# Feed-forward weight parts stored with their column blocks interleaved, the interleave changing from unit to unit

## The chip, the core and the metric

One NeuronCore of a Trainium2 chip runs the whole kernel. The metric is device time in microseconds (us) of one execution. The time of the kernel before is 2009.88 us, the median of two runs (2009.18 and 2010.57 us).

## What is computed

A trunk of two layers works on a residual stream of 512 tokens by 1024 channels, all in float32. Cut to what matters:

```python
for layer in range(2):
    h = h + 0.5 * swiglu(rms_norm(h, ffn1_g), ffn1_wg, ffn1_wu, ffn1_wd)    # 1024 -> 2816 -> 1024
    h = h + mixer(rms_norm(h, mix_g))       # layer 0: two kinds of attention; layer 1: gating and convolution
    h = h + 0.5 * swiglu(rms_norm(h, ffn2_g), ffn2_wg, ffn2_wu, ffn2_wd)
    h = h + sigmoid(rms_norm(h, ple_g) @ ple_wgate) * (p[layer] @ ple_wproj)

def swiglu(x, w_gate, w_up, w_down):
    return (silu(x @ w_gate) * (x @ w_up)) @ w_down
```

So there are four feed-forward blocks, with three weight matrices each, and they are most of the work.

## The kernel before, in words

**Three products for one.** The residual stream lies channel by channel in eight tiles `hT[k]` (128 channels by 512 tokens). A float32 product is made of three matmuls in the type float32r: each operand is split into a part that float32r holds (`hi`) and what is left (`lo`), and `mm3` (line 278; the matmuls are lines 281, 282 and 283) adds hi·hi, hi·lo and lo·hi into one bank of PSUM. In the feed-forward blocks the weights are the stationary operand (128 columns, loaded by a LDWEIGHTS in front of each matmul) and the activations are the moving one (512 columns). So `mm3` there loads `whi`, `whi` again, and `wlo`.

**Weights in units.** `wunit` (line 426) makes a `Unit` (line 383): one DMA of 1 MB brings a piece of a weight matrix into a `raw` tile (two buffers). For the gate and up matrices a unit is all 8 blocks of 128 rows by 256 columns; for the down matrix it is 4 blocks of rows by 512 columns (the last one of a group only 2 blocks). Each unit is cut into two parts of 1024 floats a partition, and `split1` (line 399) splits each part: ScalarE casts it to a `whi` tile (`acopy`, whose instruction is line 297), and VectorE subtracts that from the raw part into a `wlo` tile (`tsub`, line 321). There are six buffers of `whi` and six of `wlo`, each of 1024 floats. `pick` (line 405) gives the 128 columns of a part that a matmul takes as its stationary operand; they lie one behind the other in the buffer, at a step of 4 bytes.

**Two ways to cut a unit.** Units with 8 blocks of rows are cut by columns (`by_cols`): part 0 holds the first 128 columns of all 8 blocks, part 1 the other 128. The other units are cut by rows: part 0 holds the first half of the blocks of rows, part 1 the second half.

**Feed-forward loop** (`ffn`, line 587). For each of 11 column groups `j` there are a gate unit and an up unit, and four accumulations (gate 0, gate 1, up 0, up 1), each of 8 `mm3`. `accum` (line 558) runs the first four blocks of rows of each job that it is given, and then the second four; for `j` = 0 it is given all four jobs at once, otherwise one job after the other. Then VectorE and ScalarE multiply, apply silu and split the result into `a` tiles. After 6 and after 11 groups `down` (line 565) multiplies these by the down matrix into two groups of four banks, adds them to `hT`, and the second time feeds the next norm. `down` is also what multiplies by the output matrices of the two mixers. The very first gate and up unit are a `FirstUnit`, which loads and splits them in halves by rows.

**Order.** All instructions are recorded with an engine and an estimated cost. `Plan.order` then sets one order for each engine by a simulation with these costs and with the number of buffers of each kind (`SLOTS`, line 32; limits per stream in `CAPS`, for PSUM six of the eight banks for the main stream). An instruction that takes a new buffer waits for the last reader of the old content. Each engine works its own queue strictly in that order, and waits on semaphores where its data is not there yet.

Of the kernel before, what the change touches and what calls it, by code (L numbers as in the profile page):

```python
# [12 lines left out]
F32 = mybir.dt.float32  # L13
# [7 lines left out]
KD = D // 128  # L21
# [15 lines left out]
class Store:  # L37


    def __init__(self, tag, shape, dt, stream):  # L40
        self.tag, self.shape, self.dt, self.stream = tag, list(shape), dt, stream
        self.writer, self.readers, self.left, self.slot, self.real = None, [], 0, None, None
        self.end = 0.0


class View:
# [14 lines left out]
    def flat(self):  # L61
        p, n = self.arr.shape[0], "abc"[:self.arr.ndim - 1]
        pattern = f"p {' '.join(n)} -> p ({' '.join(n)})"
        return View(self.store, np.broadcast_to(np.False_, (p, self.n)), self.steps + (("rearrange", (pattern,)),))

    def ap(self):
        x = self.store.real
        for name, args in self.steps:
            x = getattr(x, name)(*args)
        return x  # L70

    @property
# [185 lines left out]
def trunk(ctx: ExitStack, tc: tile.TileContext, A: dict, out: bass.AP):  # L258
# [37 lines left out]
    def acopy(o, x):  # L296
        P.op("ACT", 0.83 * o.n + (52.0 if x.psum else 93.0), lambda: nc.scalar.copy(ap(o), ap(x)), w=[o], r=[x])  # L297
# [13 lines left out]
    def dve(o, fn, r, per=1.04, extra=(), fixed=0.0):  # L311
        P.op("DVE", per * o.n + 67.0 + fixed, fn, w=[o] + list(extra), r=r)
# [4 lines left out]
    def tadd(o, a, b):  # L317
        dve(o, lambda: nc.vector.tensor_add(ap(o), ap(a), ap(b)), [a, b])

    def tsub(o, a, b):  # L320
        dve(o, lambda: nc.vector.tensor_sub(ap(o), ap(a), ap(b)), [a, b])  # L321
# [23 lines left out]
    def dma(o, x, kb, after=None):  # L345
        P.op("SP", max(500.0, kb * 2.7), lambda: nc.sync.dma_start(ap(o), ap(x)), w=[o], r=[x, after],
             lat=2000.0 if isinstance(x, View) and isinstance(o, View) else 2000.0)
# [4 lines left out]
    def ps(shape=(128, S)):  # L352
        return P.tile("ps", shape)
# [29 lines left out]
    class Unit:  # L383


        def __init__(self, srcs, k, cols, by_cols):
            raw = P.tile("raw", (128, k, cols))
            for c0, c1, src in srcs:
                dma(raw[:, :, c0:c1], src, 0.5 * k * (c1 - c0))
            self.by_cols, self.half = by_cols, cols // 2 if by_cols else (k + 1) // 2  # L390
            h = self.half
            self.split([raw[:, :, h * i:h * (i + 1)] if by_cols else raw[:, h * i:h * (i + 1), :] for i in range(2)])
# [5 lines left out]

        def split1(self, r):
            hi, lo = P.tile("whi", r.arr.shape, F32R), P.tile("wlo", r.arr.shape, F32R)  # L400
            acopy(hi, r)
            tsub(lo, r, hi.bitcast(F32))
            self.parts.append((hi, lo))

        def pick(self, k, c0, n=128):
            i, r = divmod(c0 if self.by_cols else k, self.half)
            if self.by_cols:
                c0 = r
            else:
                k = r  # L410
            hi, lo = self.parts[i]
            return hi[:, k, c0:c0 + n], lo[:, k, c0:c0 + n]

    class FirstUnit(Unit):


        def __init__(self, w, cols):
            self.w, self.cols, self.by_cols, self.half, self.raw, self.parts = w, cols, False, KD // 2, [], []

        def load(self, tag):  # L420
            r = P.tile(tag, (128, self.half, self.cols))
            k0 = 128 * self.half * len(self.raw)
            dma(r, self.w[k0:k0 + 128 * self.half, 0:self.cols].rearrange("(k p) c -> p k c", p=128), 512)
            self.raw.append(r)

    def wunit(w, k0, k, c0, cols):
        src = w[128 * k0:128 * (k0 + k), c0:c0 + cols].rearrange("(k p) c -> p k c", p=128)
        return Unit([(0, cols, src)], k, cols, k == KD)


    ident = const_tile("ident", [128, 128])
# [22 lines left out]
    for part in (GAINS[:1], GAINS[1:]):  # L454
        rows = 16 * len(part)
        grow = tt(shape=(rows, 128))
        for i, name in enumerate(part):
            src = A[name].rearrange("l (k p) -> (l k) p", p=128)
            P.op("ACT", 60.0, lambda grow=grow, i=i, src=src: nc.scalar.dma_start(ap(grow[16 * i:16 * i + 16, :]), src),
                 w=[grow], lat=(3500.0, 15000.0)[len(gcol)])  # L460
        gcol.append(const_tile(f"gcol{len(gcol)}", [128, rows]))
        with P.on("norm", 60 * (len(gcol) - 1)):
            p = ps()
# [101 lines left out]
    def down(w, cats, k0, scale, norm=None):  # L565
        n = len(cats)
        for mg in range(2):
            accs = [ps() for _ in range(4)]
            for kg in range(0, n, 4):
                kk = min(4, n - kg)  # L570
                u = wunit(w, k0 + kg, kk, 512 * mg, 512)
                for k in range(kk):
                    for m in range(4):
                        mm3(accs[m], u.pick(k, 128 * m), cats[kg + k], kg + k == 0, kg + k == n - 1)
            for m in range(4):
                h = hT[4 * mg + m]
                if scale == 1.0:
                    tadd(h, accs[m], h)
                else:
                    stt(h, accs[m], scale, h, OP.mult, OP.add)  # L580
                if norm is not None:
                    norm.feed(4 * mg + m)
            if norm is not None:
                for m in range(4):
                    norm.stat(4 * mg + m)

    def ffn(pre, layer, norm, nxt, hook=None, first=None):
        xs, rcol, rb = norm.finish()
        wg, wu, wd = A[pre + "_wg"][layer], A[pre + "_wu"][layer], A[pre + "_wd"][layer]
        for j0, j1 in ((0, 6), (6, 11)):  # L590
            cats = []
            for j in range(j0, j1):
                if j == 0 and first is not None:
                    ug, uu = first
                else:
                    ug = wunit(wg, 0, KD, 256 * j, 256)
                    uu = wunit(wu, 0, KD, 256 * j, 256)
                if hook is not None and j == 7:
                    box["gate"] = cats[-1][0]
                    with P.on("hook", HOOK_BIAS):  # L600
                        hook()
                pgs, pus = [ps(), ps()], [ps(), ps()]
                jobs = [(pgs[s], ug, 128 * s) for s in range(2)] + [(pus[s], uu, 128 * s) for s in range(2)]
                if j == 0:
                    accum(xs, jobs)
                else:
                    for job in jobs:
                        accum(xs, [job])
                for pg, pu in zip(pgs, pus):
                    g, a = tt(), tt()  # L610
                    tmul(g, pg, rb)
                    act(g, g, AF.Silu)
                    tmul(a, pu, g)
                    tmul(a, a, rb)
                    cats.append(split(a, at))
            down(wd, cats, 2 * j0, 0.5, nxt if j1 == 11 else None)
# [156 lines left out]
    def even_mixer(norm, nxt, cos, sin):  # L773
        w = A["ev_w_in"][0]
# [59 lines left out]
        wv = w.rearrange("(k p) c -> p k c", p=128)  # L834

        def values(grp):
            accs = [ps() for _ in range(NT)]
            for kg in range(2):
                kw = wv[:, 4 * kg:4 * kg + 4, :]
                if grp == 0:  # L840
                    u = Unit([(0, 4, kw[:, :, 1024:1028]), (4, 258, kw[:, :, 2052:2306])], 4, 258, False)
                else:
                    u = Unit([(0, 258, kw[:, :, 2306:2564])], 4, 258, False)
                for k in range(4):
                    for t in range(NT):
                        mm3(accs[t][:, 0:258], tok(xs[4 * kg + k], t), u.pick(k, 0, 258), kg + k == 0, kg == 1 and k == 3)
            return accs
# [1 line left out]

        P.stream = "mp"  # L850
        u0 = wunit(w, 0, KD, 704, 256)
        u1 = Unit([(0, 64, wv[:, :, 512:576]), (64, 128, wv[:, :, 960:1024]), (128, 256, wv[:, :, 576:704])], KD, 256, True)
        p4 = [ps() for _ in range(4)]
        accum(xs, [(p4[0], u0, 0), (p4[1], u0, 128), (p4[2], u1, 0), (p4[3], u1, 128)])
        with P.on("side", SIDE_BIAS):
# [1 line left out]
        kk = rope(p4[2], 3, krow)  # L857
        iq = [rope(p4[0], None), rope(p4[1], None)]
        with P.on("side", SIDE_BIAS):
# [12 lines left out]
            for t in range(NT):  # L872
                p = ps()
# [11 lines left out]
        with P.on("sc", SC_BIAS):  # L885

            score = [None]
            for t in range(1, NT):
                N = 128 * (t + 1)
                sc = at()  # L890
                for h in range(4):
                    p = ps()
# [30 lines left out]
        for g in range(2):  # L923
            for j in range(2):
                u = wunit(w, 0, KD, 1028 + 512 * g + 256 * j, 256)
                for s in range(2):
                    i = 4 * g + 2 * j + s
                    p = ps()
# [45 lines left out]
        with P.on("aq", AQ_BIAS):  # L974
# [3 lines left out]
            for j in range(2):  # L978
                u = wunit(w, 0, KD, 256 * j, 256)
                for s in range(2):  # L980
                    i = 2 * j + s
                    p = ps()
# [5 lines left out]
        with P.on("pvB"):  # L988
            c = ps((128, NT, 4))
# [24 lines left out]
            v, ok, fo = small(NT, 4), small(NT, 4), small(NT, 4)  # L1014
# [3 lines left out]
            r = rsqrt(v.flat(), NT * 4, 2.0 ** -40)  # L1018
# [171 lines left out]
    n = Norm("ffn1_g", 0)  # L1190
    for k in range(KD):
        with P.on("start"):
            p = ps()
# [20 lines left out]
    n = Norm("ffn2_g", 0)  # L1214
# [3 lines left out]
    n = Norm("ffn1_g", 1)  # L1218
# [3 lines left out]
    n = Norm("ffn2_g", 1)  # L1222
# [4 lines left out]

    const.tile([128, PAD // 4], F32, name="pad")
    order = P.order()
# [7 lines left out]
TOPK_BIAS, AQ_BIAS, CONV_BIAS, CONVP_BIAS, PP_BIAS, DTAIL_BIAS, HOOK_BIAS, PE_TAPS = 2000, 450, 3000, -300, 200, -300, 400, 4  # L1237
PP0_BIAS = 600
PAD = 416
LG_BIAS, LGA_BIAS, PVA_BIAS, SIDE_BIAS, SC_BIAS = -100, -100, -300, 0, -200  # L1240
_INS = ["x", "p", "pos", "ffn1_g", "ffn1_wg", "ffn1_wu", "ffn1_wd", "mix_g", "ffn2_g", "ffn2_wg", "ffn2_wu",
        "ffn2_wd", "ple_g", "ple_wgate", "ple_wproj", "ev_w_in", "ev_w_out", "a_q_g", "a_k_g", "a_w_uv",
# [27 lines left out]
```

## Time and profile before

| what | before |
|---|---|
| median of two runs | 2009.88 us |
| the profiled execution | 2010.54 us |
| its span, first to last instruction | 2008.6 us |
| mean granted TensorE clock, share of full | 0.999 |
| PE (matmuls) busy | 1991.3 us, 99% |
| PEld (weight loads) busy | 1630.2 us, 81% |
| DVE (VectorE) busy | 1080.8 us, 54% |
| ACT (ScalarE) busy | 723.2 us, 36% |
| POOL (GpSimd) busy | 13.8 us, 1% |
| DMA | 202.28 MB, mean 101 GB/s |

The span is what the instructions of the program take; about 2 us of the execution lie around it. Busy times are unions of the recorded instructions. Weight loads have a row of their own (PEld) and run beside the matmuls; the recorded end of a matmul is modelled and overlaps the next one, so the distance between starts says more of its cost than its duration. In the rows, L281 is line 281 of the kernel, a tile's buffer number is left out (`whi` for any of the six), `128*128` is the size of the stationary operand and `128x512` that of the moving one.

### The profile page before, as it was taken

How to read it: one execution, taken by the hardware profiler on the slowest of the kernel's cores; microseconds unless marked ns; L12 is line 12 of the kernel's file. 1: busy time of each engine (PE TensorE's matmuls, PEld its weight loads, DVE VectorE, ACT ScalarE, POOL GpSimd, SP SyncE). 2: the span in 40 equal slices, each digit the busy share in tenths (PEclk: the TensorE clock that was granted, in tenths of full speed). 3: DMA queues.
4: the chain of work that ended last, by engine and by line, in shares of the span. 5: the costliest groups of instructions: out<-in, count | busy, mean ns of one | idle time of the engine just before them, and what ended most of it. 6: DMA issues, size and time to landing. Idle time of an engine off the chain costs nothing.

```text
span 2008.6 us, 22735 instructions
## 1 busy us (share of the span) xinstructions
PE 1991.3 (99%) x9154; PEld 1630.2 (81%) x9154; DVE 1080.8 (54%) x1797; ACT 723.2 (36%) x1057; POOL 13.8 (1%) x35
## 2 busy tenths in 40 slices
PE   8999999999999999999999999999999999999999
PEld 7888888888767888888888888888767888888887
DVE  6442464489986544344466443444699744334443
ACT  6322233344756422132254222223425533213232
POOL 0000000000000000000000000000000000000000
PEclk9999999999999999999999999999999999999999
DMA  5323322354330323332233322323333232323222
GB/s 189 105 97 98 108 85 84 94 160 141 96 110 22 104 86 105 94 95 95 95 121 110 105 98 92 105 75 103 107 105 105 84 97 92 105 85 104 95 104 75
DMA packets 164778, 202.28 MB, mean 101 GB/s; under 512 B 9968, under 2 KB 123072, under 8 KB 164672
## 3 DMA queue, kind: packets, MB, share of 16 engines
q1 hardware_dynamic: 164016, 200.38, 31.3%
q8 instruction: 72, 1.18, 0.2%
q0 software_dynamic: 528, 0.41, 0.2%
q14 instruction: 34, 0.28, 0.0%
q10 hardware_dynamic: 128, 0.03, 0.0%
HBM read 185.33 MB, written 6.29 MB: 95 GB/s over the span
## 4 chain that ended last, share of the span: by engine, by line
PE 97%; DVE 1%; ACT 1%; DMA 1%; issue 0%; SPq 0%; ACTq 0%; DVEq 0%
PE ps L281 30%; PE ps L282 30%; PE ps L283 30%; PE ps L276 6%; PE ps L287 1%; DMA whi<-in_x_dram 0%; ACT t L292 0%; ACT t L297 0%; DVE t L962 0%; DVE t L330 0%; DVE wlo L330 0%; DMA t<-t 0%; DVE t L309 0%; DVE wlo L321 0%; DVE a L913 0%
## 5 line engine op out<-in xcount | busy, mean ns | idle before, releaser
L297 ACT CAST whi<-raw 128x1024 fp32r<-128x1024 f32 (+2 forms) x342 | 348.7, 1022 | 976.3 <-PE ps L282 936.7
L321 DVE TENSOR_TENSOR wlo<-raw,whi 128x1024 fp32r<-128x1024 f32 (+2 forms) x342 | 405.1, 1185 | 496.8 <-ACT whi L297 496.0
L281 PE MATMUL ps<-x,whi 128*128 128x512 f32 x1664 | 655.8, 394 | 0.6 <-ACT x L297 0.6
L282 PE MATMUL ps<-x,whi 128*128 128x512 f32 x1664 | 648.7, 390 | 0.6 <-DVE x L321 0.6
L283 PE MATMUL ps<-x,wlo 128*128 128x512 f32 x1664 | 648.8, 390 | 0.0
L281 PEld LDWEIGHTS ps<-x,whi 128*128 128x128 f32 x1664 | 313.1, 188 | 66.2 <-ACT x L297 1.1
L283 PEld LDWEIGHTS ps<-x,wlo 128*128 128x128 f32 x1664 | 312.9, 188 | 65.6
L282 PEld LDWEIGHTS ps<-x,whi 128*128 128x128 f32 x1664 | 313.2, 188 | 65.1 <-DVE x L321 1.2
L281 PE MATMUL ps<-a,whi 128*128 128x512 f32 x832 | 325.1, 391 | 0.0
L282 PE MATMUL ps<-a,whi 128*128 128x512 f32 x832 | 323.9, 389 | 0.0
L283 PE MATMUL ps<-a,wlo 128*128 128x512 f32 x832 | 323.8, 389 | 0.0
L281 PEld LDWEIGHTS ps<-a,whi 128*128 128x128 f32 x832 | 156.3, 188 | 32.8 <-issue 0.5
L283 PEld LDWEIGHTS ps<-a,wlo 128*128 128x128 f32 x832 | 156.2, 188 | 32.6
L282 PEld LDWEIGHTS ps<-a,whi 128*128 128x128 f32 x832 | 156.2, 188 | 32.3 <-DVE a L321 0.7
L315 DVE TENSOR_TENSOR t<-ps,t 128x512 f32<-128x512 f32 x88 | 60.8, 691 | 209.1 <-PE ps L283 208.3
L315 DVE TENSOR_TENSOR t<-ps,rb 128x512 f32<-128x512 f32 x100 | 68.7, 687 | 112.1 <-PE ps L283 109.9
L330 DVE SCALAR_TENSOR_TENSOR a<-a 128x508 f32<-128x508 f32 (+23 forms) x108 | 72.7, 731 | 5.0 <-ACT a L292 4.6
L292 ACT ACTIVATE t<-t 128x512 f32<-128x512 f32 x100 | 62.9, 629 | 22.9 <-DVE t L315 22.8
L297 ACT CAST a<-t 128x512 fp32r<-128x512 f32 x88 | 54.8, 623 | 36.8 <-DVE t L315 36.8
L315 DVE TENSOR_TENSOR t<-t,rb 128x512 f32<-128x512 f32 x92 | 63.2, 687 | 1.2
L321 DVE TENSOR_TENSOR a<-t,a 128x512 fp32r<-128x512 f32 x88 | 60.4, 686 | 5.2 <-ACT a L297 4.8
L276 PE MATMUL ps<-a 128*128 128x512 f32 (+3 forms) x152 | 58.6, 501 | 1.5 <-ACT t L297 0.5
(167 smaller groups left out, 1358.8 us busy)
## 6 DMA issues: line engine op xcount, KB each, us to landing
raw<-in_ffn_wg_dram SPq DMA_DIRECT2D x43, 1024.0 KB, 5.1
raw<-in_ffn_wu_dram SPq DMA_DIRECT2D x43, 1024.0 KB, 5.1
raw<-in_ffn_wd_dram SPq DMA_DIRECT2D x40, 1024.0 KB, 4.9
raw<-in_ple_wgate_dram SPq DMA_DIRECT2D x8, 1024.0 KB, 5.0
raw<-in_od_w_in_dram SPq DMA_DIRECT2D x8, 1024.0 KB, 5.5
raw<-in_ev_w_in_dram SPq DMA_DIRECT2D x7, 1024.0 KB, 5.8
raw<-in_ffn_wd_dram SPq DMA_DIRECT2D x8, 512.0 KB, 3.7
raw<-in_ev_w_out_dram SPq DMA_DIRECT2D x4, 1024.0 KB, 5.3
```

The lines of the kernel that those rows point to most:

```text
L276: P.op("PE", cost, lambda: nc.tensor.matmul(ap(p), ap(a), ap(b), start=start, stop=stop), w=[p], r=[a, b], lat=160.0)
L281: nc.tensor.matmul(q, x, u, start=first, stop=False)
L282: nc.tensor.matmul(q, x, v, start=False, stop=False)
L283: return nc.tensor.matmul(q, y, u, start=False, stop=last)
L287: P.op("PE", 107.0, lambda: nc.tensor.transpose(ap(p), ap(x), ap(idn)), w=[p], r=[x, idn], lat=160.0)
L292: P.op("ACT", cost, lambda: nc.scalar.activation(ap(o), ap(x), func, scale=ap(scale), bias=ap(bias), **({"accum_out": ap(accum)} if accum ...
L297: P.op("ACT", 0.83 * o.n + (52.0 if x.psum else 93.0), lambda: nc.scalar.copy(ap(o), ap(x)), w=[o], r=[x])
L315: dve(o, lambda: nc.vector.tensor_mul(ap(o), ap(a), ap(b)), [a, b])
L321: dve(o, lambda: nc.vector.tensor_sub(ap(o), ap(a), ap(b)), [a, b])
L330: dve(o, lambda: nc.vector.scalar_tensor_tensor(ap(o), ap(a), ap(s), ap(b), op0=op0, op1=op1, **kw()), [a, s, b], extra=[accum] if accum i ...
```

## The change

A part can now be stored woven: its blocks of 128 columns are taken in groups of `s` (2, 4 or 8), and within a group the columns are interleaved, so that column `c` of block `b` lies at `c * s + b`. The cast and the subtraction write that layout (and the subtraction reads `whi` in it), while `raw` is read as it lies. A matmul's stationary operand is then 128 floats at a step of 8, 16 or 32 bytes. The list `WEAVE` says which way is used: for gate and up by `j % 4` (not woven, 2, 4, 8), for `down` by the number of the unit (2, 4, 8, not woven; units with fewer than 4 blocks of rows are not woven).

The constructor's argument `by_cols` is gone, and every unit is now cut by rows.

```diff
+    def woven(self, s, laid):
+
+        n = self.n // (128 * s)
+        order = "n s c" if laid else "n c s"
+        return View(self.store, np.broadcast_to(np.False_, (self.arr.shape[0], n, s, 128)),
+                    self.steps + (("weave", (f"p ({order}) -> p n s c", n, s)),))
...
-        def __init__(self, srcs, k, cols, by_cols):
+        def __init__(self, srcs, k, cols, weave):
+            self.weave = weave
+            by_cols = False
...
         def split1(self, r):
             hi, lo = P.tile("whi", r.arr.shape, F32R), P.tile("wlo", r.arr.shape, F32R)
-            acopy(hi, r)
-            tsub(lo, r, hi.bitcast(F32))
+            if self.weave is None:
+                acopy(hi, r)
+                tsub(lo, r, hi.bitcast(F32))
+            else:
+                s = self.weave
+                x, h, l = r.flat().woven(s, True), hi.flat().woven(s, False), lo.flat().woven(s, False)
+                acopy(h, x)
+                tsub(l, x, h.bitcast(F32))
             self.parts.append((hi, lo))
...
-            return hi[:, k, c0:c0 + n], lo[:, k, c0:c0 + n]
+            if self.weave is None:
+                return hi[:, k, c0:c0 + n], lo[:, k, c0:c0 + n]
+            i, j = divmod((hi.arr.shape[2] * k + c0) // 128, self.weave)
+            return tuple(v.flat().woven(self.weave, False)[:, i, j, :] for v in (hi, lo))
...
-    def wunit(w, k0, k, c0, cols):
+    def wunit(w, k0, k, c0, cols, weave=None):
         src = w[128 * k0:128 * (k0 + k), c0:c0 + cols].rearrange("(k p) c -> p k c", p=128)
-        return Unit([(0, cols, src)], k, cols, k == KD)
+        return Unit([(0, cols, src)], k, cols, weave)
...
-                u = wunit(w, k0 + kg, kk, 512 * mg, 512)
+                u = wunit(w, k0 + kg, kk, 512 * mg, 512, WEAVE[1][(k0 + kg) // 4 % 4] if kk == 4 else None)
...
-                    ug = wunit(wg, 0, KD, 256 * j, 256)
-                    uu = wunit(wu, 0, KD, 256 * j, 256)
+                    ug = wunit(wg, 0, KD, 256 * j, 256, WEAVE[0][j % 4])
+                    uu = wunit(wu, 0, KD, 256 * j, 256, WEAVE[0][j % 4])
...
+WEAVE = [[None, 2, 4, 8], [2, 4, 8, None]]
```

## Rows read from the trace of the kernel before

**Rows 1.** The page: span, busy times, granted clock by slice, chain that ended last.
```profile
span 2008.6 us, 22735 instructions
PE 1991.3 (99%) x9154; PEld 1630.2 (81%) x9154; DVE 1080.8 (54%) x1797; ACT 723.2 (36%) x1057; POOL 13.8 (1%) x35
...
PEclk9999999999999999999999999999999999999999
...
PE 97%; DVE 1%; ACT 1%; DMA 1%; issue 0%; SPq 0%; ACTq 0%; DVEq 0%
PE ps L281 30%; PE ps L282 30%; PE ps L283 30%; PE ps L276 6%; PE ps L287 1%; DMA whi<-in_x_dram 0%; ACT t L292 0%; ACT t L297 0%; DVE t L962 0%; DVE t L330 0%; DVE wlo L330 0%; DMA t<-t 0%; DVE t L309 0%; DVE wlo L321 0%; DVE a L913 0%
```
**Rows 2.** Windows: length, busy us (instructions) by engine, granted clock, DMA share, GB/s.
```profile
30.00:220.00 190.00, 190.00 (x842) 157.38 (x841) 79.11 (x94) 53.42 (x62) 5.02 (x10) 1.00 0.32 105
380.00:660.00 280.00, 273.77 (x1532) 219.23 (x1531) 228.64 (x653) 153.60 (x332) 4.33 (x8) 1.00 0.36 105
1604.00:1965.00 361.00, 361.00 (x1597) 298.98 (x1597) 156.35 (x192) 108.53 (x132) 0.00 (x0) 1.00 0.31 100
```
**Rows 3.** Timeline, PE, inside a down product: start and length, us.
```profile
200.09 0.39 PE L283 MATMUL ps<-a,wlo 128*128 128x512 f32 x1
...
202.81 0.39 PE L283 MATMUL ps<-a,wlo 128*128 128x512 f32 x1
```
**Rows 4.** Timeline, PEld, the same stretch.
```profile
200.10 0.19 PEld L281 LDWEIGHTS ps<-a,whi 128*128 128x128 f32 x1
200.32 0.19 PEld L282 LDWEIGHTS ps<-a,whi 128*128 128x128 f32 x1
```
**Rows 5.** Instruction groups, PE and PEld: count, busy us, mean ns, idle before.
```profile
L281 PE MATMUL ps<-x,whi 128*128 128x512 f32 x1664 | 655.8, 394 | 0.6 <-ACT x L297 0.6
L281 PE MATMUL ps<-a,whi 128*128 128x512 f32 x832 | 325.1, 391 | 0.0
...
L281 PEld LDWEIGHTS ps<-x,whi 128*128 128x128 f32 x1664 | 313.1, 188 | 66.2 <-ACT x L297 1.1 <-issue 0.7 <-DVE t L325 0.3
...
L287 PEld LDWEIGHTS ps<-ident,t 128*128 128x128 f32 x156 | 18.3, 141 | 7.8 <-issue 2.8 <-ACT t L292 1.4 <-DVE t L330 0.6
...
L276 PEld LDWEIGHTS ps<-t,a 128*64 128x64 f32 x160 | 13.0, 136 | 8.5 <-DVE t L309 3.7 <-ACT t L297 1.8 <-DVE s L962 0.9
...
L276 PEld LDWEIGHTS ps<-t,a 128*128 128x128 f32 x80 | 10.9, 191 | 2.8 <-ACT t L297 1.2 <-issue 0.5
```
**Rows 6.** Timeline, PEld, a run of matmuls with one moving column.
```profile
381.72 0.86 PEld L276 LDWEIGHTS ps<-ones,rb 128*128 128x128 f32 x7
```
**Rows 7.** Instruction groups, ACT and DVE: making the parts, emptying PSUM.
```profile
L321 DVE TENSOR_TENSOR wlo<-raw,whi 128x1024 fp32r<-128x1024 f32 x318 | 388.6, 1223 | 483.6 <-ACT whi L297 482.7
L297 ACT CAST whi<-raw 128x1024 fp32r<-128x1024 f32 x318 | 333.8, 1052 | 935.5 <-PE ps L282 895.8 <-PE ps L283 17.8 <-issue 13.1
...
L315 DVE TENSOR_TENSOR t<-ps,t 128x512 f32<-128x512 f32 x88 | 60.8, 691 | 209.1 <-PE ps L283 208.3 <-ACT t L292 0.7
...
L330 DVE SCALAR_TENSOR_TENSOR h<-ps,h 128x512 f32<-128x512 f32 x64 | 42.6, 689 | 14.1 <-PE ps L283 14.1
```
**Rows 8.** Waits: us in total, times, longest us.
```profile
ACT whi L297 <- PE ps L282: 936.7, 261, 11.4
...
DVE t L315 <- PE ps L283: 318.3, 128, 5.6
```
**Rows 9.** Timeline, DVE, around the step between two halves of a down product.
```profile
173.54 1.22 DVE L321 TENSOR_TENSOR wlo<-raw,whi 128x1024 fp32r<-128x1024 f32 x1 [4.21 <-ACT whi L297]
176.04 2.73 DVE L330 SCALAR_TENSOR_TENSOR h<-ps,h 128x512 f32<-128x512 f32 x4 [1.27 <-PE ps L283]
178.94 1.23 DVE L321 TENSOR_TENSOR wlo<-raw,whi 128x1024 fp32r<-128x1024 f32 x1 [0.17 <-ACT whi L297]
```

More of the change, by code (lines that the diff above doesn't have):

```diff
@@ L68, in ap @@
         for name, args in self.steps:
-            x = getattr(x, name)(*args)
+            if name == "weave":
+                x = x.rearrange(args[0], n=args[1], s=args[2], c=128)
+            else:
+                x = getattr(x, name)(*args)
         return x
@@ L400, in split1 @@
             hi, lo = P.tile("whi", r.arr.shape, F32R), P.tile("wlo", r.arr.shape, F32R)
-            acopy(hi, r)
-            tsub(lo, r, hi.bitcast(F32))
+            if self.weave is None:
+                acopy(hi, r)
+                tsub(lo, r, hi.bitcast(F32))
+            else:
+                s = self.weave
+                x, h, l = r.flat().woven(s, True), hi.flat().woven(s, False), lo.flat().woven(s, False)
+                acopy(h, x)
+                tsub(l, x, h.bitcast(F32))
             self.parts.append((hi, lo))
@@ L418, in __init__ @@
             self.w, self.cols, self.by_cols, self.half, self.raw, self.parts = w, cols, False, KD // 2, [], []
+            self.weave = None
         def load(self, tag):
@@ L840, in values @@
                 if grp == 0:
-                    u = Unit([(0, 4, kw[:, :, 1024:1028]), (4, 258, kw[:, :, 2052:2306])], 4, 258, False)
+                    u = Unit([(0, 4, kw[:, :, 1024:1028]), (4, 258, kw[:, :, 2052:2306])], 4, 258, None)
                 else:
-                    u = Unit([(0, 258, kw[:, :, 2306:2564])], 4, 258, False)
+                    u = Unit([(0, 258, kw[:, :, 2306:2564])], 4, 258, None)
                 for k in range(4):
@@ L851, in even_mixer @@
         u0 = wunit(w, 0, KD, 704, 256)
-        u1 = Unit([(0, 64, wv[:, :, 512:576]), (64, 128, wv[:, :, 960:1024]), (128, 256, wv[:, :, 576:704])], KD, 256, True)
+        u1 = Unit([(0, 64, wv[:, :, 512:576]), (64, 128, wv[:, :, 960:1024]), (128, 256, wv[:, :, 576:704])], KD, 256, None)
         p4 = [ps() for _ in range(4)]
```

## The prediction

> **What bounds the kernel now.** I read the page first: PE is busy 99% of the span, the granted clock is at full speed (2.4 GHz) in every slice, and the chain that ended last is 97% PE, nine tenths of it the three lines of `mm3` [rows 1]. So only what changes the distance between matmuls, or makes PE wait, counts. The windows come second: inside the feed-forward blocks PE has no idle time (190.00 of 190.00 us, 842 matmuls), DVE is busy 42% and ACT 28%; in the even mixer PE idles 6 us of 280 and DVE is busy 82% [rows 2].
>
> The timeline then gives the price of one matmul. Twelve steps lie between the two starts shown, 2.72 us, so one float32r matmul of 512 columns takes 226.7 ns from start to start [rows 3]; 190 us over 842 gives 225.7 with the few short ones in it [rows 2]. 512 columns at 2.4 GHz would be 213.3, so 13.4 ns are on top. A weight load starts about 10 ns after the matmul before its own [rows 3, 4] and is recorded with 188 ns [rows 5]. How much of that occupies the load path? A load of 64 columns is recorded with 136 ns, so a column takes (188 - 136) / 64 = 0.81 ns, 128 columns 104 ns, and some 84 ns are latency [rows 5]. Where the moving operand has one column, seven loads fill 0.86 us, so one follows the other after (0.86 - 0.19) / 6 = 112 ns [rows 6]: that is the least period that a load sets, 104 ns of reading and 8 around it. Today the load needs 112 to 122 ns (with the 10 ns of lag) out of 226.7, and is hidden.
>
> **The change, part by part.**
>
> *Which loads change.* Per feed-forward block, `j` % 4 leaves 3 of 11 column groups as they are, 3 have step 8, 3 step 16 and 2 step 32; a group is two units, 96 matmuls. In `down` a full unit has 48 matmuls, and the numbers of the units give, for both column halves, 4 units of step 8, 2 of step 16 and 2 of step 32 per block. The four `down` calls of the mixers go through the same line: 4 units of step 8 and 4 of step 16 in all. Sum: step 8: 4 x 3 x 96 + 16 x 48 + 4 x 48 = 2112 matmuls; step 16: 1152 + 384 + 192 = 1728; step 32: 768 + 384 = 1152; 4992 of the 7488 in these groups (3 x (1664 + 832)) [rows 5]. No matmul, load or byte of DMA is added.
>
> *A load at a step.* No row shows one, so I bound it. From below it costs nothing; a gain can't exceed the 13.4 ns above the columns [rows 3]. From above, if all words between were read too, step 8 takes 2 x 104 ns, step 16 4 x 104, step 32 8 x 104. The period would be 112 + (k - 1) x 104 ns, plus at most 10 of lag, where k is the factor on the reading. k = 2 gives 216 to 226 ns, just under 226.7: hidden. k = 3 gives 320 to 330, k = 4 424 to 434, k = 8 840 to 850. So the whole question is whether the reading at step 16 and 32 takes more than about 2.05 times as long as now. The nearest row is the load in the transposes (L287): the same 128 columns with 141 ns, 47 less than 188, which leaves 57 ns of reading, 0.45 ns a column [rows 5]. It is another kind of load, but it shows that words can come nearly twice as fast as `whi` asks for them; a path with that reserve can lose half its rate and the load is as now. I take k between 1 and 2 for all three steps, because a halved rate is the mildest penalty and two mild ones in a row would still be hidden: 0 us.
>
> [...]
>
> *Casting and subtracting into the woven layout.* Of the 318 parts of 1024, 88 become step 8, 72 step 16 and 48 step 32 (four or two parts per group or unit as counted above). A cast takes 1052 ns and a subtraction 1223 [rows 7]. No row has an operand at a step; lower bound no change, upper bound three times the part that goes with the columns (the whole above some 200 ns): 2.8 and 3.3 us. I take a doubling of that part for steps 16 and 32 and nothing for step 8: +0.86 and +1.08 us on 120 parts, 103 us of ACT and 130 us of DVE, which lifts them to 41% and 60% of the span [rows 1]. What hides it: ACT waits for PE to give up a buffer before 261 casts, 937 us in all [rows 8], so a part is made as soon as the oldest of six buffers is free. A part feeds 24 matmuls, 5.44 us, so five parts or 27 us lie before its use, against 2.3 us now, 4.2 with my value and 6.1 at the upper bound.
>
> The cost that can show is in the queues: whatever stands behind a longer subtraction on DVE, above all what empties PSUM. In the gate and up loop two of six banks are spare, 10.9 us of cover. Between the halves of a down product it is tighter: the four updates of `hT` run from 176.04 us on, one every 0.69 us, and the subtraction before them began at 173.54 [rows 9]. At the upper bound it would begin 1.7 us later and last 3.3, to 178.6, and the first bank come free at 179.3. The third accumulation of the next half wants it 2.04 + 1.36 us after 176.04, at 179.4: still hidden, with nothing to spare; where the next norm is fed in between (once per block), up to a microsecond may show. In the even mixer, with DVE at 82% [rows 2], four parts of step 16 add 4 x 1.08 = 4.3 us to DVE and may show in full. I take +4 us for all of this, between 0 and 15.
>
> *All units cut by rows.* Gate and up units need both parts within 2.7 us of the first matmul instead of 5.4, and give them up at 8.2 and 10.9 us instead of 5.4 and 10.9. With three units in six buffers the next use is still some 22 us off, so this is hidden by the same cover. The instruction count is the same. But the planner sets all queues anew, also where nothing is woven; where PE waits at all (6 us in the even mixer [rows 2]) this can go either way, -5 to +5 us. I take 0.
>
> **Sum.** 0 + 4 + 0 = +4 us on the profiled execution of 2010.54 us, which is 0.7 us above the median 2009.88; on the median 2014 us.
>
> **Rivals.**
>
> B, *the load becomes the bound.* One column at step 16 or 32 takes three times as long as now. Then 2880 matmuls go from 226.7 to some 325 ns: 2880 x 98 = 282 us, 2292 us. It decides from k = 2.05 on, at 4.7 us for each further 0.016 (1.6 ns a matmul). For it: the margin at k = 2 is no more than 0 to 10 ns. Against: the faster loads of L287. [...]
>
> C, *only a part of B.* Step 32 alone goes to k = 3 (1152 x 98 = 113 us, 2123 us), or a halved rate meets the 213 ns of the moving operand and adds 10 ns on 2880 (29 us, 2039 us). Between 2030 and 2150.
>
> D, *worse.* The words in between are read (k = 4 at step 16: 1728 x 202 = 349 us, k = 8 at step 32: 1152 x 618 = 712 us), or step 8 pays as well: 2450 us and more.
>
> E, *the subtractions come late.* The upper bound on DVE and ACT, with a stall of a few us at each of the some 20 joints between products: 2050 us.
>
> F, *faster.* Some of the 13.4 ns comes from reading weights and activations at the same time, and the other addresses avoid it: at most 4992 x 13.4 = 67 us, 1943 us. Nothing in the rows speaks for it: the 13.4 ns are the same in both kinds of product.
>
> **How the numbers follow.** The forecast (all loads hidden, 2000 to 2030 us) gets 0.62, B 0.17, C 0.11, D 0.04, E 0.02, F 0.04. About 2% (40 us) is what a measurement of this kernel tells from no change: faster 0.04; within it the 0.62 and the low end of C, 0.64; slower 0.32. The range has to take in B, because forecast, C and E alone leave a quarter out: from 1998 (forecast with a lucky order) to 2310 (B with its lag). The forecast's own range is 2000 to 2030.
>
> **What would show it.** Right: weight loads of `whi` and `wlo` with groups of 188 ns beside longer ones, none over about 300 (84 + 2 x 104), matmul starts still 226.7 ns apart at every step, PE idle below 20 us, casts and subtractions of two or three lengths up to 1.9 and 2.3 us, and ACT's wait for PE shorter by what the casts grew. B: starts some 325 ns apart and loads near 400 ns in the units of step 16 and 32 and unchanged ones in the rest. E: PE idle before L281 ended by `wlo` or by a bank. The forecast is wrong if starts are over 231 ns apart in any woven unit, or if PE's waits grow by more than 20 us.

## The result, and the profile after

The changed kernel takes 2075.1 us (median of two runs, 2075.02 to 2075.18) against 2009.88: the ratio is 1.032, with a 95% interval of 1.030 to 1.034. It is slower by 65 us. That lies inside the range, but only because the range had been drawn out to take in rivals C and B (up to 2310 us); it is outside the forecast's own 2000 to 2030, and the +4 us of the sum were 65.

The page of the kernel after; its lines stand ten higher from `mm3` on (L281 to L283 are now L291 to L293, L297 is L307, L321 is L331):

```profile
span 2073.2 us, 22760 instructions
PE 2047.8 (99%) x9154; PEld 1793.3 (87%) x9154; DVE 1196.1 (58%) x1802; ACT 860.8 (42%) x1053; POOL 13.8 (1%) x35
...
PEclk9999999999999999999999999999999999999999
...
PE 93%; DVE 4%; DMA 1%; ACT 1%; issue 1%; SPq 0%; DVEq 0%; ACTq 0%
```

Beside [rows 1]: as many matmuls, the same clock (0.998 of full on the mean, 0.999 before), PE busy 99% as before, and 65 us more. The matmuls themselves follow each other more slowly (233 to 244 ns in woven units, against 226.7). The chain has 4% of DVE in it where there was 1%: something waits for VectorE now. Windows split the two. First the even mixer, then a whole feed-forward block (the second of four), then the odd mixer; columns as in [rows 2]. Before the change:

```profile
373.50:651.00 277.50, 271.27 (x1517) 216.80 (x1516) 227.88 (x653) 153.51 (x333) 4.33 (x8) 1.00 0.36 106
651.00:1011.30 360.30, 360.30 (x1597) 298.43 (x1596) 155.29 (x191) 108.30 (x133) 0.00 (x0) 1.00 0.29 95
...
1416.70:1595.50 178.80, 177.83 (x764) 134.67 (x763) 151.91 (x241) 80.31 (x119) 0.40 (x4) 0.99 0.31 104
```

And after it:

```profile
385.00:675.00 290.00, 278.22 (x1518) 225.61 (x1517) 234.28 (x658) 156.19 (x329) 4.33 (x8) 0.99 0.35 101
675.00:1047.00 372.00, 372.00 (x1597) 335.62 (x1596) 181.38 (x192) 140.76 (x133) 0.00 (x0) 1.00 0.29 92
...
1464.00:1648.40 184.40, 180.75 (x762) 140.92 (x762) 155.63 (x241) 84.48 (x119) 0.41 (x4) 0.98 0.30 100
```

The first and the last weight matmul of a block in the timeline give the limits. A block went from 360.2 to 371.9 us with the same 1597 matmuls and no idle PE (the first, with its start-up, from 363.5 to 375.1); the even mixer from 277.5 to 290.0, the odd from 178.8 to 184.6, both with more PE idle. So 46.5 us come from the four blocks and 18.3 from the two mixers: 64.8, and the spans differ by 64.6.

Inside a block the units can be told apart. Windows of 21 us in column groups 1 to 4 of the first block: step 8, 16, 32 bytes, not woven.

```profile
37.00:58.00 21.00, 21.00 (x92) 17.37 (x91) 12.93 (x14) 10.91 (x10) 0.00 (x0) 1.00 0.33 101
59.50:80.50 21.00, 21.00 (x91) 21.00 (x90) 13.83 (x13) 9.61 (x8) 0.00 (x0) 1.00 0.31 101
82.00:103.00 21.00, 21.00 (x87) 21.00 (x87) 8.34 (x12) 6.04 (x8) 0.00 (x0) 1.00 0.30 100
105.00:126.00 21.00, 21.00 (x94) 17.41 (x93) 9.82 (x12) 6.64 (x8) 1.96 (x4) 1.00 0.31 101
```

In the second and third PEld has no gap left (21.00 of 21.00 us), so the load may be the bound there; the sweep below tests it. In the first it has gaps, as in the fourth (17.37 and 17.41 us busy), and yet fewer matmuls fit (92 against 94). The weight loads of these windows, in the same order (mean ns after the bar):

```profile
L292 PEld LDWEIGHTS ps<-x,whi 128*128 128x128 f32 x31 | 6.0, 193 | 1.2
...
L292 PEld LDWEIGHTS ps<-x,whi 128*128 128x128 f32 x30 | 9.3, 310 | 0.0
...
L292 PEld LDWEIGHTS ps<-x,whi 128*128 128x128 f32 x29 | 9.6, 329 | 0.0
...
L292 PEld LDWEIGHTS ps<-x,whi 128*128 128x128 f32 x31 | 5.8, 188 | 1.2
```

188 ns is the value of [rows 5]. Taken from start to start over all units, a matmul takes 226.7 ns where the load has no step, 233.3 at 8 bytes, 235.0 at 16 and 244.4 at 32. With the counts of the prediction (without the mixers' matrices): 1920 x 6.6 + 1536 x 8.3 + 1152 x 17.7 ns = 12.7 + 12.7 + 20.4 = 45.8 us. That is nearly all of the blocks' 46.5.

### The profile page after: what moved, and what is told of

Same layout as the page of the kernel before. It is cut to its first block, busy times and chain, and to the rows that moved or that the text cites. A ratio compares the mean times of both kernels' runs of the same rounds, so it can differ in the third digit from the quotient of the medians.

```text
span 2073.2 us, 22760 instructions
## 1 busy us (share of the span) xinstructions
PE 2047.8 (99%) x9154; PEld 1793.3 (87%) x9154; DVE 1196.1 (58%) x1802; ACT 860.8 (42%) x1053; POOL 13.8 (1%) x35
## 4 chain that ended last, share of the span: by engine, by line
PE 93%; DVE 4%; DMA 1%; ACT 1%; issue 1%; SPq 0%; DVEq 0%; ACTq 0%
PE ps L291 29%; PE ps L292 29%; PE ps L293 29%; PE ps L286 5%; PE ps L297 1%; DVE wlo L331 1%; ACT t L302 0%; DVE a L935 0%; DVE t L984 0%; DVE m L934 0%; SPq L356 0%; DMA whi<-in_x_dram 0%; DMA t<-in_a_w_uv_dram 0%; DVE t L340 0%; DMA t<-t 0%
## 5 line engine op out<-in xcount | busy, mean ns | idle before, releaser
L331 DVE TENSOR_TENSOR wlo<-raw,whi 128x1024 fp32r<-128x1024 f32 (+2 forms) x342 | 513.8, 1503 | 544.5 <-ACT whi L307 544.0
L307 ACT CAST whi<-raw 128x1024 fp32r<-128x1024 f32 (+2 forms) x342 | 484.1, 1419 | 549.2 <-PE ps L292 522.3
L291 PE MATMUL ps<-x,whi 128*128 128x512 f32 x1664 | 667.7, 401 | 1.9 <-ACT x L307 1.9
L292 PE MATMUL ps<-x,whi 128*128 128x512 f32 x1664 | 659.7, 396 | 0.2 <-DVE x L331 0.2
L293 PE MATMUL ps<-x,wlo 128*128 128x512 f32 x1664 | 659.2, 396 | 0.0
L291 PEld LDWEIGHTS ps<-x,whi 128*128 128x128 f32 x1664 | 398.7, 240 | 43.9 <-ACT x L307 2.4
L292 PEld LDWEIGHTS ps<-x,whi 128*128 128x128 f32 x1664 | 398.9, 240 | 41.3 <-issue 1.7
L293 PEld LDWEIGHTS ps<-x,wlo 128*128 128x128 f32 x1664 | 398.7, 240 | 41.3
L291 PE MATMUL ps<-a,whi 128*128 128x512 f32 x832 | 331.6, 399 | 0.0
L292 PE MATMUL ps<-a,whi 128*128 128x512 f32 x832 | 329.1, 396 | 0.0
L293 PE MATMUL ps<-a,wlo 128*128 128x512 f32 x832 | 329.0, 395 | 0.0
L291 PEld LDWEIGHTS ps<-a,whi 128*128 128x128 f32 x832 | 199.0, 239 | 21.4 <-issue 0.9
L292 PEld LDWEIGHTS ps<-a,whi 128*128 128x128 f32 x832 | 199.4, 240 | 20.3
L293 PEld LDWEIGHTS ps<-a,wlo 128*128 128x128 f32 x832 | 199.2, 239 | 20.4
L331 DVE TENSOR_TENSOR a<-t,a 128x512 fp32r<-128x512 f32 x88 | 60.6, 689 | 35.7 <-ACT a L307 35.7
L340 DVE SCALAR_TENSOR_TENSOR a<-a 128x506 f32<-128x506 f32 (+22 forms) x108 | 73.0, 726 | 5.2 <-ACT a L302 4.8
L307 ACT CAST a<-t 128x512 fp32r<-128x512 f32 x88 | 54.7, 622 | 39.5 <-DVE t L325 39.5
```

The lines of the kernel that those rows point to most:

```text
L291: nc.tensor.matmul(q, x, u, start=first, stop=False)
L292: nc.tensor.matmul(q, x, v, start=False, stop=False)
L293: return nc.tensor.matmul(q, y, u, start=False, stop=last)
L340: dve(o, lambda: nc.vector.scalar_tensor_tensor(ap(o), ap(a), ap(s), ap(b), op0=op0, op1=op1, **kw()), [a, s, b], extra=[accum] if accum i ...
```

## The experiments

Two theories on the step: L, the load alone takes longer and becomes the bound; S, the load and the moving operand are read at the same time and delay each other. And on the mixers: the new order of the queues (theory A of the first run), or parts that are made too late (theory B). The changed kernel and the runs without a step, with storing alone, with reading alone and with step 8 bytes everywhere put the instructions of PE, VectorE and ScalarE in the same order, so between these five only the layouts differ.

**Cut by rows, nothing woven.**

```diff
-WEAVE = [[None, 2, 4, 8], [2, 4, 8, None]]
+WEAVE = [[None] * 4, [None] * 4]
```

> Every unit is cut by rows as in the changed kernel, but none is woven. Theory A (the step of the weight loads costs the time in the feed-forward blocks, +11.7 us each, and the new order of the queues the rest): the four blocks fall back to 360.2 us each, matmul starts 226.7 ns apart everywhere, and the mixers keep what they lost, so 2010 + 15 = 2025 us. Theory B (the mixers lose because casts and subtractions at a step are late there): all of it goes, 2007 to 2014 us.

2018.26 us against 2011.01 of the kernel before on the same chip, ratio 1.004 (1.003 to 1.005): +7 us, between the two numbers. Windows of the second block and the even mixer:

```profile
373.30:655.00 281.70, 274.02 (x1517) 217.92 (x1517) 230.90 (x658) 151.94 (x328) 4.34 (x8) 1.00 0.36 104
655.00:1015.30 360.30, 360.30 (x1597) 298.43 (x1596) 157.04 (x191) 109.25 (x133) 0.00 (x0) 1.00 0.30 95
```

The blocks are back at 360.2 us; the even mixer keeps 4.2 us of its 12.5, the odd one 1.2 of 5.8. So the row cut with its new order costs some 5 to 7 us, nearly all of it outside the blocks (the first one takes 0.7 us more), and what the mixers lose beyond that needs the steps.

**Woven in the feed-forward blocks alone**, other units of 8 blocks cut by columns again.

```diff
-            by_cols = False
+            by_cols = k == KD and weave is None
...
-..., WEAVE[1][(k0 + kg) // 4 % 4] if kk == 4 else None)
+..., WEAVE[1][(k0 + kg) // 4 % 4] if kk == 4 and ff else None)
```

> Woven as in the changed kernel in the feed-forward blocks alone; the output matrices of the mixers are not woven, and units of 8 blocks that are not woven are cut by columns as before. Theory A: feed-forward blocks at 371.9 us each as in the changed kernel, mixers close to the kernel before (277.5 and 178.8 us), 2010 + 47 = 2057 us. Theory B: the same time, because no part at a step is made in the mixers; the two are told apart by the other run. A third, that the loss in the mixers follows from any new order by chance: mixers off by some 10 us either way, 2045 to 2070 us.

2057.63 us, ratio 1.023 (1.022 to 1.025), the time that both theories gave. Blocks at 371.9 us, mixers at 278.3 and 180.4. The blocks' loss does not depend on what else was changed.

**Stored woven, read as it lies.**

```diff
         def pick(self, k, c0, n=128):
...
-            if self.weave is None:
-                return hi[:, k, c0:c0 + n], lo[:, k, c0:c0 + n]
-            i, j = divmod((hi.arr.shape[2] * k + c0) // 128, self.weave)
-            return tuple(v.flat().woven(self.weave, False)[:, i, j, :] for v in (hi, lo))
+            return hi[:, k, c0:c0 + n], lo[:, k, c0:c0 + n]
```

> Parts are stored woven as in the changed kernel, but every matmul reads 128 words in a row, so the products of woven units are taken with the wrong weights; instructions and waits are those of the changed kernel. If reading at a step is the cost: weight loads all 188 ns, starts 226.7 ns apart, blocks at 360.2 us, casts still 1.13, 2.06 and 2.23 us, and only the mixers' share remains: 2022 to 2027 us. If storing at a step is (ScalarE's and VectorE's accesses slowing TensorE's reads, or late parts): the blocks stay at 366 us or more, over 2045 us.

2025.92 us, +15, ratio 1.007 (1.005 to 1.010). A window of the second block and its loads:

```profile
659.80:1020.00 360.20, 360.20 (x1596) 298.38 (x1595) 179.88 (x191) 139.15 (x133) 0.00 (x0) 1.00 0.30 95
...
L292 PEld LDWEIGHTS ps<-x,whi 128*128 128x128 f32 x352 | 66.1, 188 | 13.6
```

DVE is as busy as in the changed kernel (180 us of 360) and PE as fast as before the change: storing at a step, and the longer casts and subtractions, cost nothing in the blocks (one of four has a stall of 1.6 us). In the mixers the run takes 286.3 and 183.8 us, 4.6 and 3.8 more than with nothing woven.

**Stored as it lies, read at a step.**

```diff
-            if self.weave is None:
+            if True:
                 acopy(hi, r)
                 tsub(lo, r, hi.bitcast(F32))
```

> Parts are stored as they lie, by casts and subtractions of the old length, and the matmuls of the units that the changed kernel weaves read at the same steps as there, so they multiply the wrong words. Theory (reading at a step costs the time in the blocks; the late casts cost some 8 us in the mixers; the new order some 7): blocks at 371.9 us each, mixers between those of the run with nothing woven and those of the changed kernel, 2010 + 47 + 3 + 7 = 2067 us. If storing at a step had a share in the blocks: below 2055 us.

2068.4 us, ratio 1.028 (1.026 to 1.030). Blocks at 371.9 us (375.8 the first), mixers at 285.2 and 181.0, which is 3.5 and 1.0 above nothing woven. In the mixers the order then costs 4.2 + 1.2, reading 3.5 + 1.0, storing 4.6 + 3.8, in all 18.3 us, and the changed kernel lost 18.3 there.

That close a sum is in part luck, and the split of the mixers is not shown. Each figure comes from one execution, while the ten times of the run with nothing woven lie between 2016 and 2026 us. And the clock differs: the write-only run has a granted clock of 0.50 for 6.8 us of the even mixer and 10.2 of the odd, the changed kernel for 3.4 and 6.8, the read-only run for 3.4 and 3.4, the kernel before and the run with nothing woven for 0 and 3.4. The first such stretch of the changed kernel came right after one in which PE worked only 1.39 of 3.40 us:

```profile
615.70:619.10 3.40, 1.39 (x7) 0.83 (x8) 2.78 (x16) 3.20 (x11) 0.00 (x0) 1.00 0.73 222
619.10:622.50 3.40, 3.40 (x16) 2.68 (x16) 1.94 (x9) 1.66 (x6) 0.00 (x0) 0.50 0.25 89
```

An estimate from the 0.50: where PE sets the pace, half of such a stretch is lost, so up to 6.8 of the 8.4 us put to storing can be the clock, and up to 1.7 of the 4.5 put to reading. The blocks are free of this: the granted clock is 1.00 in every window of a feed-forward block read here.

**A sweep of the load's step, with four kinds of moving operand.**

```diff
+    def swept(f, v, p, u, xs):
+        st, off = SWEEP[v]
+        for k in range(KD):
+            a = []
+            for t in u.parts[k // u.half]:
+                t = t.flat()
+                a.append(t[:, off:off + 127 * st + 1:st] if st else t[:, off:off + 1].to_broadcast([128, 128]))
+            b, q = xs[k], p
+            if f == 1:
+                b = tuple(x[:, 0:1].to_broadcast([128, S]) for x in b)
+            if f >= 2 and k >= KD // 2:
+                n = 2 if f == 2 else 256
+                b, q = tuple(x[:, 0:n] for x in b), p[:, 0:n]
+            mm3(q, a, b, k == 0, k == KD - 1)
```

> Nothing is stored woven. In the gate and up accumulations of all column groups but the first, each of 40 accumulations per block has a step of its own (0 to 8 words, from a start 0 to 3 words into the part, and four more starts), so these products are wrong. Block 1: as in the kernel otherwise. Block 2: the moving operand is one column read 512 times. Block 3: the second four of the eight blocks of rows with 2 moving columns. Block 4: these with 256. Theory L (the load alone takes longer at steps of 4 words and more, and is the bound): the pairs with 2 columns follow each other at 112 ns up to step 2, at some 230 at step 4 and 245 at step 8; block 2 shows the same periods as block 1. Theory S (load and moving operand delay each other in reading): with 2 columns the loads at step 4 and 8 follow at 112 to 216 ns; in block 2 the periods fall, towards 216 ns, and the more so the larger the step; with 256 columns the extra time over 107 + 13 ns is the same as with 512. Step 0 under S: 216 to 220 ns in block 1; under L: 226.7. [...]

The timeline of PE gives the distances. Four pairs of rows, each the first and the last of a run: block 1 with step 1, 23 steps apart; block 2 with step 2 words, also 23; block 3 with step 1 and with step 4 words, each 10 apart.

```profile
58.44 0.39 PE L291 MATMUL ps<-x,whi 128*128 128x512 f32 x1
...
63.66 0.40 PE L293 MATMUL ps<-x,wlo 128*128 128x512 f32 x1
...
732.26 0.38 PE L291 MATMUL ps<-x,whi 128*128 128x512 f32 x1
...
737.22 0.38 PE L293 MATMUL ps<-x,wlo 128*128 128x512 f32 x1
...
1112.77 0.25 PE L292 MATMUL ps<-x,whi 128*128 128x2 f32 x1
...
1113.89 0.25 PE L293 MATMUL ps<-x,wlo 128*128 128x2 f32 x1
...
1169.02 0.37 PE L292 MATMUL ps<-x,whi 128*128 128x2 f32 x1
...
1171.36 0.37 PE L293 MATMUL ps<-x,wlo 128*128 128x2 f32 x1
```

5.22 / 23 = 227 ns, 4.96 / 23 = 216, 1.12 / 10 = 112 and 2.34 / 10 = 234. Read in this way at full resolution, ns from start to start, all with loads that begin at the first word of the part (the granted clock is full in these stretches, but 0.93 for the load alone at step 8):

| step, words (bytes) | load alone (2 columns) | 512 columns, one word over and over | 512 columns |
|---|---|---|---|
| 0 | 111.6 | 215.8 | 231.3 |
| 1 (4) | 111.6 | 215.8 | 226.7 |
| 2 (8) | 117.8 | 215.8 | 232.7 |
| 3 (12) | 175.2 | 215.9 | 235.2 |
| 4 (16) | 233.6 | 233.3 | 235.2 |
| 5 (20) | 219.7 | 220.0 | 237.8 |
| 6 (24) | 221.8 | 222.3 | 237.3 |
| 7 (28) | 229.9 | 230.0 | 238.8 |
| 8 (32) | 237.8 | 237.8 | 246.6 |

The middle column is the larger of 215.8 and the left one, everywhere, to within 0.5 ns. That is theory L: from step 4 on the load alone (219.7 to 237.8 ns) takes longer than a matmul with one moving word and a load in a row (215.8). The right column is more than the middle one, everywhere, by 2 to 19 ns. That is theory S, and it holds at step 1 too: 226.7 against 215.8. Both are true, in different units. S, as it was expected, failed in several points. The loads alone are as L had them (233.6 and 237.8 ns). With the moving operand at one word the times fall, but not the more the larger the step (10.9 ns at step 1, 16.9 at 2, 1.9 at 4). Step 0 came out as neither theory had it, at 231.3. And with 256 columns, step 1 and step 2 follow at 119.9 and 119.3 ns, so the 6 ns of step 2 are not there; but as the loads alone take 112 and 118 ns and the 256 columns only 107 (an estimate: 512 columns at step 1 take 226.7 and 256 take 119.9, so a column 0.417 ns), that test says little about a load that has time to spare.

**What of the moving operand it is.**

```diff
+        if kind in (1, 2, 9):
+            a, b = {1: (4, 128), 2: (32, 16), 9: (128, 4)}[kind]
+            return x[:, 0:b][:, None, :].to_broadcast([128, a, b])
+        if kind in (3, 4):
+            a, b = {3: (256, 2), 4: (128, 4)}[kind]
+            return x[:, 0:a][:, :, None].to_broadcast([128, a, b])
```

> Nothing is stored woven; in the gate and up accumulations of all column groups but the first the operands are other words than the product needs, so these products are wrong. Block 1: loads of 128 words in a row from a start 0, 4, ... 156 words into the part. Block 2: 472 moving columns from a start 0 to 39 words into the tile. Block 3: both starts, 8 by 5. Block 4: ten ways to read the moving operand (0: 512 in a row, 1: 128 words four times, 2: 16 words 32 times, 3: each of 256 words twice, 4: each of 128 words four times, 5: 256 at a step of 2 words, 6: 128 at a step of 4, 7: 256 in a row, 8: one word 512 times, 9: four words 128 times), each with loads at step 1, 2, 4 and 8. Theory S (loads and moving operand get in each other's way in reading, and that is most of the 13.4 ns above the columns): ways that bring a new 16 bytes less often (3, 4, 8, 9) fall to 216 ns at step 1 and 2, ways 1 and 2 stay at 227 and 233 like way 0. Rival (the 13.4 ns are a start-up of the moving stream, the same whatever is loaded): 216 ns only in way 8, where nothing new is read at all, and the extra time of step 2 is as large in ways 3, 4 and 9 as in way 0. [...]

Two runs at load step 2 words, 11 steps each, from the timeline of PE: 512 columns in a row, then 256 words, each read twice.

```profile
1619.72 0.39 PE L297 MATMUL ps<-x,whi 128*128 128x512 f32 x1
...
1622.29 0.40 PE L299 MATMUL ps<-x,wlo 128*128 128x512 f32 x1
...
1687.61 0.38 PE L297 MATMUL ps<-x,whi 128*128 128x512 f32 x1
...
1689.99 0.38 PE L299 MATMUL ps<-x,wlo 128*128 128x512 f32 x1
```

2.57 / 11 = 234 ns against 2.38 / 11 = 216, with as many columns and the same load. All seven ways with 512 columns, by step of the load in words:

| moving operand | step 1 | 2 | 4 | 8 |
|---|---|---|---|---|
| 512 words in a row | 226.6 | 233.4 | 234.9 | 244.4 |
| 128 words, four times | 226.6 | 233.3 | 234.8 | 244.4 |
| 16 words, 32 times | 242.4 | 244.2 | 241.7 | 240.8 |
| each of 256 words twice | 215.7 | 215.8 | 237.2 | 241.1 |
| each of 128 words four times | 215.8 | 215.7 | 234.6 | 245.9 |
| 4 words, 128 times | 215.8 | 215.8 | 233.2 | 237.7 |
| one word, 512 times | 215.8 | 215.7 | 233.4 | 237.7 |

The rival (a fixed start-up of the moving stream) falls: with half as many new words in a stretch of time, or with only four words in all, the extra time is gone at steps 1 and 2. So 10.9 ns (226.7 less 215.8) of the some 13 above the columns (512 at 0.417 ns are 213.6), and the whole 6.6 ns of step 8 bytes, need a moving operand that brings new words at its full rate. That the load has its part in it is shown for what its layout adds: its step (226.7 to 246.6 ns) and its start (226.6 to 234.3) alone move the time. For the 10.9 ns it is inferred, because every matmul of these runs has a load. At steps 4 and 8 a slower moving operand does not always help (245.9 ns at a quarter of the rate), and 16 words read 32 times, which the theory expected at 227 and 233 ns, took 242 and 244.

Starts did not help: with step 1 the load's start gave 226.6 ns at 0, 4, 60, 64, 68, 124, 128 and 132 words and 228.8 to 234.3 at the others, and 472 columns took 210.0 to 220.1 ns from any start, never less than 13.1 above the 196.9 that 0.417 ns a column would give. So most starts cost about as much at step 1 as step 8 bytes does (233.3): the kernel before has the good ones, multiples of 128 words. Of the three ways with fewer columns one tells something of the moving operand: 256 columns at a step of 8 bytes take 230 ns with loads in a row, and 256 in a row 120. I found no layout that beats the kernel before.

**Step 8 bytes everywhere.**

```diff
-WEAVE = [[None, 2, 4, 8], [2, 4, 8, None]]
+WEAVE = [[2] * 4, [2] * 4]
```

> Every unit that the changed kernel can weave is woven with 2 blocks (step of 8 bytes): 6432 matmuls. If each costs 6.6 ns more, as in the units of step 8 bytes of the changed kernel, +42 us, and the new order 8: 2060 us, hardly less than with steps mixed although the loads alone are as fast as before. If step 8 bytes is only slow where units of step 16 and 32 are being made beside it: near 2018 us, the time with nothing woven.

2066.49 us, ratio 1.026 (1.025 to 1.028): but for the 5 to 7 us of the row cut the step costs this, with loads that alone would take only 6 ns longer (117.8 against 111.6) and no subtraction longer than before (1.23 us at step 8 bytes in the changed kernel, 1.22 before), and 6 us more than I had worked out. The windows of 290 us, in the second and the third block, show why:

```profile
710.00:1000.00 290.00, 290.00 (x1233) 242.00 (x1232) 118.35 (x138) 81.81 (x91) 0.00 (x0) 1.00 0.28 90
1110.00:1400.00 290.00, 290.00 (x1245) 239.87 (x1244) 120.68 (x141) 83.41 (x93) 0.00 (x0) 1.00 0.28 93
```

The same matmuls take 235.6 ns in the second and fourth block and 233.3 in the first and third. In the changed kernel, with its instructions in the same order, the units of step 8 bytes take 233.3 in all four. What sets which of the two it is was not tried.

## Why the prediction was right or wrong

The forecast failed, by its own sign: starts over 231 ns apart in a woven unit (233 to 244 were measured), and loads recorded with more than 300 ns (310 and 329). That the time lies in the range is owed to the rivals for which it was made wide, and as far as the forecast goes it is luck: B's mechanism, loads three times as slow, did not come, and of C a part did.

*What bounds the kernel*: right. Only the distance of matmuls counts; PE is not idle in the windows of the blocks, before (360.30 of 360.30 us) or after (372.00 of 372.00). The 213.3 ns for 512 columns stand on a pace of 2.4 columns a ns, which the sweep bears out: by its 226.7 and 119.9 ns for 512 and 256 columns, a column takes 0.417 ns, 512 take 213.6, and 13.1 ns are on top (an estimate).

*A load at a step*: here it failed. The formula, 112 + (k - 1) x 104 ns, and the deciding point, k = 2.05, hold: the loads alone follow at 117.8, 233.6 and 237.8 ns, which is k = 1.06, 2.17 and 2.21. But "I take k between 1 and 2 for all three steps", which made the term 0 us, was on the wrong side of that point for steps 16 and 32, and in the blocks the term measured 46.5 us. The fast loads of the transposes proved no reserve for these. That a halved rate is the mildest penalty, and that two would still be hidden, was an assumption, and the runs show otherwise: step 8 bytes leaves the load nearly as it was (117.8 against 111.6 ns), while step 16 doubles its reading (from 104 to some 226 ns, an estimate from the 233.6 less the 8 around it), and that is no longer hidden (233.6 against 226.7). By the formula alone these loads would have given 1536 x 7 + 1152 x 11 ns = 23 us in the blocks.

The other half has its root in the first part. I read 13.4 ns above the columns and took them as fixed in the forecast, and a load that ends in time as free. It is not: with step 8 bytes, where the load had 100 ns to spare (117.8 ns of 226.7), each matmul takes 6.6 ns more, and that goes, with 10.9 of the 13.4, when the moving operand brings fewer new words (215.8 ns). Reading both at once is the likely cause, which no row shows directly. It is not the step as such that sets this price, since at step 1 most starts cost about as much (228.8 to 234.3 ns). Rival F named this mechanism, and allowed it only to get better. That the load's layout alone moves the time, 233.3 against 226.7 ns, is what these runs show for it.

*Casting and subtracting*: sizes about right. The casts take 1.13, 2.06 and 2.23 us, the subtractions 1.23, 2.03 and 2.26 (predicted up to 1.9 and 2.3); ACT grew by 138 us and DVE by 115, against 103 and 130. Two casts of the kernel after, for steps 16 and 32 bytes, from the timeline of ACT, and ACT's wait for PE there and with nothing woven:

```profile
47.49 2.06 ACT L307 CAST whi<-raw 128x1024 fp32r<-128x1024 f32 x1 [0.54 <-PE ps L292]
...
55.88 2.20 ACT L307 CAST whi<-raw 128x1024 fp32r<-128x1024 f32 x1
```

```profile
ACT whi L307 <- PE ps L292: 522.3, 235, 5.0
...
ACT whi L307 <- PE ps L292: 579.2, 231, 6.2
```

The wait shrank from 937 us [rows 8] to 522 and never ran out in the blocks: the cover held, as the run that only stores woven shows. It did not shrink by what the casts grew, as I had expected: with nothing woven it is 579 us, so 358 of the 415 us went with the new order. In the mixers I had +4 us, and the run that only stores woven lost 8.4 there, the odd mixer included, which I had left out; how much of that is the clock and how much late parts stays open.

*All units cut by rows*: 0 taken, within -5 to +5; 5 to 7 us by the run with nothing woven, a little outside, and mostly in the even mixer, where it was looked for.

*Rivals*: C came nearest, in time (2030 to 2150 us) and by its second half, a load that meets the matmul's time; but it had step 16 and 32 alone, and a quarter of the blocks' loss is step 8. B's three-fold reading, which would have given some 325 ns a matmul, no run shows: at steps 16 and 32 bytes the loads alone took 233.6 and 237.8 ns, the matmuls 235.0 and 244.4. D's 2450 us does not follow from its own two terms, which would give 3071.

## What to carry to other kernels

A weight load that ends before its matmul is due need not be free while the moving operand is read at full rate: its layout moved the time here by 6.6 ns a matmul, so look at what the starts are above the columns' own time (here 226.7 ns for 512 columns at 0.417, some 13 ns above) before calling a load hidden. Keep stationary operands of 4-byte words in a row, and mind where they start (226.6 or up to 234 ns here); at steps of 16 to 32 bytes the load alone (219.7 to 237.8 ns) outlasted 512 columns of one word (215.8). Where a new layout lengthens work on other engines, price it in the stretches where PE waits (here the mixers), not by the engines' totals, and read the granted clock of these stretches (0.50 for up to 10.2 us of a mixer here) before putting a loss to a cause.

## What was not expected of the hardware

A step of 20 or 24 bytes loads faster than one of 16 (219.7 and 221.8 against 233.6 ns), and a load of one word 128 times makes the matmul slower than a load in a row (231.3 against 226.7, both from the first word of the part), though alone it takes as long (111.6). Sixteen moving words read 32 times are the slowest way of all with step 1 (242.4 ns), four words 128 times one of the fastest (215.8). Distances fall into a fixed rhythm (226, 227, 227 ns in the kernel before and in units that are not woven, 231, 240, 231, 238 in units of step 16 bytes of the kernel after), and with step 8 bytes everywhere the same matmuls ran two whole blocks at 233.3 ns and two at 235.6. What the reads contend for is not settled by these runs; only that the load's layout counts (226.7 or 233.3 ns), and that at steps 1 and 2 the extra time goes when the moving operand brings fewer new words (215.7 or 215.8).
